# A two-layer hybrid trunk step on one core: bank pools of the FFN's products, the place of the residual sums and of LN1's last sums, small copies on ScalarE, an RMS root by ln and exp

## The chip, the cores and the metric

The kernel runs on one core of a Trainium2 chip. A core has five engines with a queue each: TensorE (PE, with its weight loads PEld), VectorE (DVE), ScalarE (ACT), GpSimd (POOL) and SyncE (SP). Each engine works its queue off in order; what an instruction needs from another engine it waits for on semaphores. The metric is the device time of one execution in microseconds.

## The reference, cut to what matters

One inference step of a decoder trunk of two layers, in fp32, on 1024 tokens of a new sequence and 8 x 4 sample tokens that continue from given states:

```python
for l in range(DEPTH):
    p = x @ w_in[l]
    p_rw, p_gl, p_rt = _split(p, (RWKV_COLS, GLA_COLS, RET_COLS))
    y_a, sh, s_a = _rwkv7_mix(p_rw, ...)      # 6 heads of 64
    y_b, s_b = _gla_mix(p_gl, ...)            # 5 heads, then _rms_heads, gate
    y_c, s_c = _ret_mix(p_rt, ...)            # 5 heads, then _rms_heads, gate
    mix = jnp.concatenate([y_a, y_b, y_c], axis=-1) @ w_out[l]
    x = _layer_norm(ALPHA * x + mix, ln1_g[l], ln1_b[l])
    f, cv = _conv_ffn(x, ...)
    x = _layer_norm(ALPHA * x + f, ln2_g[l], ln2_b[l])

def _rms_heads(o):
    return o * lax.rsqrt(jnp.mean(jnp.square(o), -1, keepdims=True) + RMS_EPS)

def _conv_ffn(x, conv0, w_up, conv_w, conv_b, w_down):
    u = x @ w_up                                             # 1024 -> 2 x 2816
    buf = jnp.concatenate([conv0.astype(u.dtype), u], axis=1)
    c = conv_b + sum(conv_w[j] * buf[:, j:j + t_] for j in range(CONV_W))   # 3 taps in time
    a, b = jnp.split(c, 2, axis=-1)
    return (jax.nn.gelu(a) * b) @ w_down, buf[:, -(CONV_W - 1):]
```

## The kernel before

**Tiles.** The 1056 tokens lie in three blocks of 384, 384 and 288 columns (the last holds 32 sample tokens and 256 prompt tokens); channels lie on partitions. An fp32 product is three matmuls (`mm3`, L130): each operand is a high part, cast on ACT, and a low part, the difference, taken mostly on POOL (`split`, L187). So a weight tile `wir` or `wU0r` becomes `...wh` (ACT) and `...wl` (POOL).

**Stages of a layer.** First the RWKV stage (chains of small products, `gps`, `tps`, `zy`), then the GLA and RetNet stage with the output projection (`ytp` turns the heads' outputs, `po` projects) and LayerNorm 1, then the FFN and LayerNorm 2. The input products of the GLA and RetNet columns (`gt`) are filler for PE in the first two stages.

**Who sets the order.** PE's order is written out at build time: generators (streams) yield either a delay from the table `AFTER` or an event, a clock `TE.t` adds up the matmuls' nominal time, and a stream goes on when its delay is over on that clock; meanwhile filler is issued. PE's instructions are chained in that order (`Tensor.order`). The queues of the other engines are ordered by the framework's scheduler, from its own simulation.

**LayerNorm 1.** Per block, `ln.add` sums a tile and its square on DVE and POOL (L931, L932), `ln.stats` has PE sum over the partitions (`lnm`, `lnv`), and `ln.apply` makes the normed block: DVE subtracts the mean (L956), takes the variance (L946), ACT makes the root by ln and exp (L947, L948, each with a table load here), DVE multiplies (L957), ACT scales (L958), and ACT and POOL split the result into `x1h` and `x1l`.

**RMS root.** `finish` takes an output of GLA or RetNet (`gop`, `rop`): ACT copies it and squares it, DVE sums per head (L976), and `rsqrt` (L228 to L234) makes the root on DVE in twelve operations on 128 x 5 values: a bit trick and three Newton steps. Then L980 and L981 multiply. There are 36 calls of `finish` in the program and 18 other calls of `rsqrt`, in the RWKV stage.

**FFN.** The 22 pairs of up tiles go two by two. Pairs 0 and 1 (`up_blocks`, products `pu`) are plain: per block, two tiles of 48 matmuls together. Then `residual` (L1442) puts `x1h + x1l` together in fp32 on POOL, sixteen 128 x 384 additions, and `sums` makes from these the operands of a scheme of seven products for four (blocks 0 and 1 times two weight halves). From pair 2 on, `up` runs the seven products `pa`, `pg`, `pb`, `pc`, `pf`, `pd`, `pe` and the sample block's `p0`, `p1`. The first product's tile `u` is added to the second, `pg`, by DVE at L1524; on `u` the three taps run (L1402 on ACT, L1398 on DVE), then gelu (L1431) and the gate (L1432), then the split into `hh` and `hl`. Behind `pg` of every second pair stand the `downs` of the two pairs before: 24 products `pd` of two pairs each, added to `acc` by DVE (L1594; the first group L1596). A down of block 0 or 1 is six matmuls, and the first four of a half are block 0's, the next four block 1's.

**Banks.** In the FFN PSUM has two pools: `pd` with five banks (all seven products and the downs) and `pg` with three (`pu` of blocks 0 and 1, `p0`, `p1`). A tile of a pool takes the banks in turn and waits until the bank's last reader is done.

**Halos.** The first two columns of a `u` are the last two of the tile before it in time (POOL copy L1394), or zero (POOL memset L1391), or come from the convolution's given state (`cvt`, POOL copy L1415).

**FFN weights.** They go through six buffers for `wh` and six for `wl`. Pair 0 has four pieces (`wU0`), so two of pair 1's (`wU1`) can be split at once and the others when PE gives up the first pieces.

Of the kernel before, what the change touches and what calls it, by code (L numbers as in the profile page):

```python
# [159 lines left out]
def step_kernel(ctx: ExitStack, tc: tile.TileContext, xT, wA, wB, wO, wU, wD, pp, pb, lora, bg, bgk, shT, cvT, srw, sgl, srt,  # L160
# [136 lines left out]
    for l in range(depth):  # L297
# [1090 lines left out]
        def halo(u, n, prev):  # L1388

            if n == 0:  # L1390
                G.memset(u[:, 0:2], 0.0)  # L1391
            else:
                o = 48 if n == 2 else 0
                G.tensor_copy(u[:, o:o + 2], prev[:, 384:386])  # L1394

        def taps(t, c, uu, cv, w):
            for tap in (1, 0):
                V.scalar_tensor_tensor(cv, uu[..., tap:tap + w], pc(PP_CV + 4 * t + tap), cv, ALU.mult, ALU.add)  # L1398
# [6 lines left out]
        def conv_prompt(t, i, u, src):  # L1405

            c = conv_start(t, i, src, 384)
            taps(t, c, u[:, 0:386], c, 384)
            return c

        def conv_samples(t, i, ps):
# [3 lines left out]
            G.tensor_copy(s[:, :, 0:2], cvt[:, t, 2:18].rearrange("p (b t) -> p b t", b=8))  # L1415
# [413 lines left out]
```

## Time and profile before

| | |
|---|---|
| median of 3 runs | 3508.7 us (3494.66 to 3511.85) |
| profiled execution, own time | 3504.8 us |
| its span | 3503.0 us |
| mean granted clock of TensorE | 0.936 |
| PE busy, 0 to 600 us | 554.97 us |
| PE busy, 600 to 916 us (GLA, RetNet, output, layer 0) | 276.27 of 316 us |
| PE busy, 916 to 1016 us (FFN entry, layer 0) | 81.28 of 100 us |
| PE busy, 1016 to 1700 us (FFN, layer 0) | 652.07 of 684 us |
| PE busy, 2650 to 2750 us (FFN entry, layer 1) | 79.18 of 100 us |
| PE busy, 2750 to 3450 us (FFN, layer 1) | 666.26 of 700 us |

A row of waits names the engine, the tile and line that waited, what it waited for, the total in us, how often, and the longest. In a timeline a bracket holds the idle time ahead of an instruction and what ended it.

### The profile page before, as it was taken

What the parts mean: (1) busy time and instruction counts of PE and PEld (TensorE: products, weight loads), DVE (VectorE), ACT (ScalarE), POOL (GpSimd) and SP (SyncE); (2) the same over time, 40 slices, a digit from 0 to 9 for tenths busy, and PEclk for the clock granted to TensorE, in tenths of its full rate; (3) what the DMA queues carried; (4) which work ended last, traced back from release to release, by engine and by line L of the source; (5) the groups of instructions that cost most, each with busy time, mean ns of one, the idle gap of its engine ahead of it and who ended that gap; (6) DMA issues with size and microseconds to landing.
All of it is one profiled execution on the core that took longest, in us unless ns stands there. A gap on an engine that the chain in (4) does not pass through costs nothing.

```text
span 3503.0 us, 59691 instructions
## 1 busy us (share of the span) xinstructions
PE 3184.6 (91%) x21630; PEld 2937.8 (84%) x21630; DVE 2445.3 (70%) x5493; ACT 1492.9 (43%) x3286; POOL 1680.2 (48%) x1876
## 2 busy tenths in 40 slices
PE   9889999988799999999888999999887999999995
PEld 8778888777799899989787888877777989999995
DVE  3587664677687767677946776647777786777778
ACT  6554332334543334333575533323345433433335
POOL 5442222133665555554765422221437655655566
PEclk9789999998999999999898899999898999999998
DMA  7343223343311111111264422243432111111111
GB/s 247 116 122 92 64 61 125 116 122 99 84 40 47 42 46 49 46 40 46 80 192 143 118 79 65 69 127 119 129 98 70 43 43 45 47 46 42 46 52 66
DMA packets 245570, 291.17 MB, mean 83 GB/s; under 512 B 76620, under 2 KB 158316, under 8 KB 245276
## 3 DMA queue, kind: packets, MB, share of 16 engines
q1 hardware_dynamic: 225004, 274.08, 25.7%
q10 hardware_dynamic: 20272, 13.29, 1.5%
q8 instruction: 170, 2.79, 0.3%
q14 instruction: 124, 1.02, 0.1%
HBM read 228.85 MB, written 58.43 MB: 82 GB/s over the span
## 4 chain that ended last, share of the span: by engine, by line
PE 52%; DVE 22%; POOL 7%; DMA 7%; issue 5%; ACT 4%; SPq 1%; ACTq 0%; DVEq 0%; POOLq 0%
PE pd L130 11%; PE gt L130 9%; PE pa L130 6%; PE p L130 4%; DVE c L1398 3%; DVE tm L622 2%; DVE U L624 2%; PE pb L130 2%; PE po L130 2%; PE gps L130 2%; DVE c L1432 2%; PE zy L130 1%; PE pf L130 1%; PE pc L130 1%; PE gop L130 1%
## 5 line engine op out<-in xcount | busy, mean ns | idle before, releaser
L1398 DVE SCALAR_TENSOR_TENSOR c<-u,ppt,c 128x32 f32<-128x32 f32 (+2 forms) x704 | 489.4, 731 | 145.2 <-ACT u L1416 64.1
L187 POOL TENSOR_TENSOR wil<-wir,wih 128x512 fp32r<-128x512 f32 (+1 forms) x264 | 368.1, 1402 | 352.9 <-ACT wih L187 342.2
L130 PE MATMUL gt<-wih,xh 128*128 128x320 f32 (+1 forms) x1008 | 341.3, 340 | 0.0
L130 PE MATMUL gt<-wil,xh 128*128 128x320 f32 (+1 forms) x1008 | 317.1, 316 | 6.6 <-POOL wil L187 6.6
L1594 DVE TENSOR_TENSOR acc<-acc,pd 128x384 f32<-128x384 f32 (+1 forms) x464 | 230.8, 516 | 98.8 <-PE pd L130 98.7
L130 PE MATMUL gt<-wih,xl 128*128 128x320 f32 x896 | 282.3, 315 | 0.0
L187 ACT CAST wih<-wir 128x512 fp32r<-128x512 f32 (+1 forms) x296 | 185.6, 637 | 166.6 <-PE po L130 69.6
L130 PE MATMUL pa<-xh,wih 128*128 128x384 f32 (+1 forms) x576 | 217.9, 378 | 19.3 <-DVE mx L380 8.8
L622 DVE TENSOR_TENSOR tm<-U,N 96x60 f32<-96x60 f32 (+24 forms) x558 | 176.4, 316 | 65.4 <-DMA N<-gd 46.4
L130 PEld LDWEIGHTS gt<-wih,xh 128*128 128x128 f32 (+1 forms) x1008 | 187.9, 186 | 37.0 <-issue 21.2
L130 PE MATMUL pa<-xl,wih 128*128 128x384 f32 (+1 forms) x576 | 203.0, 352 | 3.9 <-POOL xl L187 3.6
L130 PE MATMUL pa<-xh,wil 128*128 128x384 f32 (+1 forms) x576 | 202.4, 351 | 4.2 <-POOL wil L187 3.5
L130 PEld LDWEIGHTS gt<-wil,xh 128*128 128x128 f32 (+1 forms) x1008 | 189.4, 188 | 10.7 <-POOL wil L187 9.5
L624 DVE TENSOR_TENSOR U<-U,tm 96x60 f32<-96x60 f32 (+24 forms) x558 | 171.3, 307 | 14.4 <-DMA tokd<-ev 0.4
L130 PEld LDWEIGHTS gt<-wih,xl 128*128 128x128 f32 x896 | 173.9, 194 | 0.0
L1402 ACT ACTIVATE c<-u,ppt 128x384 f32<-128x384 f32 x160 | 113.2, 709 | 108.0 <-DVE u L1524 38.0
L187 POOL TENSOR_TENSOR hl<-c,hh 128x384 fp32r<-128x384 f32 x132 | 143.2, 1090 | 22.8 <-ACT hh L187 22.8
L130 PEld LDWEIGHTS pa<-xh,wih 128*128 128x128 f32 x576 | 121.2, 210 | 33.4 <-DVE mx L380 10.3
L130 PE MATMUL po<-yh,wih 128*128 128x384 f32 (+1 forms) x384 | 137.3, 358 | 13.0 <-DVE ac L1317 9.3
L130 PE MATMUL po<-yh,wil 128*128 128x384 f32 (+1 forms) x384 | 130.4, 339 | 3.8 <-DVE wil L187 3.8
L130 PE MATMUL po<-yl,wih 128*128 128x384 f32 (+1 forms) x384 | 130.1, 339 | 0.0
L130 PEld LDWEIGHTS pa<-xl,wih 128*128 128x128 f32 x576 | 121.8, 211 | 9.0 <-POOL xl L187 5.8
(955 smaller groups left out, 10425.3 us busy)
## 6 DMA issues: line engine op xcount, KB each, us to landing
wir<-in_wA_dram SPq DMA_DIRECT2D x144, 256.0 KB
wir<-in_wO_dram SPq DMA_DIRECT2D x96, 256.0 KB
wir<-in_wB_dram SPq DMA_DIRECT2D x56, 320.0 KB
tokd<-ev SPq DMA_DIRECT2D x112, 160.0 KB
x<-rkvd SPq DMA_DIRECT2D x16, 576.0 KB
tk<-tokd SPq DMA_DIRECT2D x16, 480.0 KB
rkvd<-mx SPq DMA_DIRECT2D x36, 192.0 KB
tk<-tokd SPq DMA_DIRECT2D x16, 400.0 KB
```

Source lines behind the costliest of these rows:

```text
L130: self.order(self.engine.matmul(out, lhsT, rhs, start=start, stop=stop), cols, 4 if rhs.dtype == F32 else 1)
L187: return A.copy(dst_h, src), (le or G).tensor_tensor(dst_l, src, dst_h.bitcast(F32), ALU.subtract)
L622: V.tensor_tensor(tm, U[:, 0:nr, i:i + 1].to_broadcast([4 * ns, nr, 31 - i]), N[:, i:i + 1, i + 1:32].to_broadcast([4 * ns, nr, 31 - i]), ...
L624: V.tensor_tensor(U[:, 0:nr, i + 1:32], U[:, 0:nr, i + 1:32], tm, ALU.add)
L1398: V.scalar_tensor_tensor(cv, uu[..., tap:tap + w], pc(PP_CV + 4 * t + tap), cv, ALU.mult, ALU.add)
L1402: A.activation(c, src, AF.Identity, scale=pc(PP_CV + 4 * t + 2), bias=pc(PP_CV + 4 * t + 3))
L1432: V.tensor_tensor(cs[1], cs[0], cs[1], ALU.mult)
L1594: V.tensor_tensor(a, a, ps, ALU.add)
```

## The change

It has these parts:

1. In `up` the second product `pg` takes its bank from the pool of three, with `p0` and `p1`; in `up_blocks` the products of blocks 0 and 1 take theirs from the pool of five, and those of block 2 from the pool of three.
2. `residual` is issued at the start of the second pair, after that pair's weights, not after the first pair's block 1.
3. The zero halo is left out: the two taps that reach before the sequence run on 383 and 382 columns. The other halos and the copy from the convolution's state go from POOL to ACT.
4. `finish` has ACT load a table set (`natural_log_exp_and_others`) behind the square, then take ln and exp of the sums. `rsqrt` stays for the RWKV stage.
5. LN1's sums over partitions of block 2 (`lnm`, `lnv`) are held back and put on PE behind the first pair's block 0, with no delay ahead of them.
6. In the planner's table, `operands` gets 5.5 more for blocks 0 and 1, and `x11` goes from 1.28 to 3.0.
7. LN2's sums take their banks from the pool of three in all blocks.

```diff
-AFTER = {... "operands": 8.0, ... "x11": 1.28, ...}
+AFTER = {... "operands": 8.0, "early": 5.5, ... "x11": 3.0, ...}
...
     def order(self, ins, cols, passes):
+        if self.held is not None:
+            self.held.append((ins, cols, passes))
+            return
...
+    def hold(self, do):
+
+        self.held = []
+        do()
+        held, self.held = self.held, None
+        return lambda: [self.order(*h) for h in held]
...
-            yield AFTER["operands"]
+            yield AFTER["operands"] + (AFTER["early"] if s.b < 2 else 0)
...
-            A.activation(sq, dst, AF.Square)
+            first = A.activation(sq, dst, AF.Square)
...
             V.tensor_reduce(sm, hv(sq), mybir.AxisListType.X, ALU.add)
-            sm = rsqrt(gp_, sm, 1.0 / 64, 1e-6)
+
+            ins = TE.after(A.preload_act_table_set("natural_log_exp_and_others"), first)
+            TE.after(A.activation(sm, sm, AF.Ln, scale=1.0 / 64, bias=eps(1, rows)), ins)
+            A.activation(sm, sm, AF.Exp, scale=-0.5)
...
-            yield AFTER["ln"]
-            ln.stats()
+            yield AFTER["ln"] if n < 2 else 0
+            if n < 2:
+                ln.stats()
+            else:
+                stats3.append(TE.hold(ln.stats))
...
         def halo(u, n, prev):
 
-            if n == 0:
-                G.memset(u[:, 0:2], 0.0)
-            else:
+            if n:
                 o = 48 if n == 2 else 0
-                G.tensor_copy(u[:, o:o + 2], prev[:, 384:386])
+                A.copy(u[:, o:o + 2], prev[:, 384:386])
 
-        def taps(t, c, uu, cv, w):
+        def taps(t, c, uu, cv, w, first=False):
             for tap in (1, 0):
-                V.scalar_tensor_tensor(cv, uu[..., tap:tap + w], pc(PP_CV + 4 * t + tap), cv, ALU.mult, ALU.add)
+                o = 2 - tap if first else 0
+                V.scalar_tensor_tensor(cv[..., o:], uu[..., tap + o:tap + w], pc(PP_CV + 4 * t + tap), cv[..., o:], ALU.mult, ALU.add)
...
-            G.tensor_copy(s[:, :, 0:2], cvt[:, t, 2:18].rearrange("p (b t) -> p b t", b=8))
+            A.copy(s[:, :, 0:2], cvt[:, t, 2:18].rearrange("p (b t) -> p b t", b=8))
...
         def up_blocks(j):
...
+            if j:
+                residual()
             for n in range(3):
...
-                    ps = bank(2, f"pu{t}")[:, :NB[n][1]] if n == 2 else pg.tile([P, 512], F32, tag="g", name=f"pu{t}")[:, :384]
+                    ps = bank(n, f"pu{t}")
...
-                if n == 1:
-                    qs = sums() if j else residual()
+                if n == 0 and j == 0:
+                    stats3[0]()
+                if n == 1 and j:
+                    qs = sums()
...
-            p2 = bank(0, "pg")
+            p2 = pg.tile([P, 512], F32, tag="g", name="pg")[:, :384]
             product(p2, w, b21)
             u11 = new_u()
-            halo(u11, 0, None)
...
-                lns[n].ps = lambda name: pg.tile([P, 512], F32, tag="g", name=name)
...
-            lns.append(LayerNorm(n, acc[n], (t[:, 0], t[:, 1]), lambda name: pd.tile([P, 512], F32, tag="d", name=name), (fp, "u", 6)))
+            lns.append(LayerNorm(n, acc[n], (t[:, 0], t[:, 1]), lambda name: pg.tile([P, 512], F32, tag="g", name=name), (fp, "u", 6)))
```

What the change does to the queues is not all to be seen in the code. Three places follow. The first is PE in layer 0, the fourth and the fifth down behind `pg` of pair 4 (weights of pairs 2 and 3; the brackets name the engines that a matmul waits for). Before:

```order
L130 MATMUL pd<-hh,wD2wh 128x384 [waits Activation_49]
L130 MATMUL pd<-hl,wD2wh 128x384
L130 MATMUL pd<-hh,wD2wl 128x384
L130 MATMUL pd<-hh,wD3wh 128x384
L130 MATMUL pd<-hl,wD3wh 128x384
L130 MATMUL pd<-hh,wD3wl 128x384
L130 MATMUL pd<-hh,wD2wh 128x384 [waits DVE_49]
L130 MATMUL pd<-hl,wD2wh 128x384
L130 MATMUL pd<-hh,wD2wl 128x384
L130 MATMUL pd<-hh,wD3wh 128x384 [waits Activation_49]
L130 MATMUL pd<-hl,wD3wh 128x384 [waits Pool_49]
L130 MATMUL pd<-hh,wD3wl 128x384
```

The fourth down takes the bank of `pa`, which ACT frees, the fifth that of `pg`, which DVE frees. The same two downs in the changed kernel:

```order
L140 MATMUL pd<-hh,wD2wh 128x384 [waits DVE_49]
L140 MATMUL pd<-hl,wD2wh 128x384
L140 MATMUL pd<-hh,wD2wl 128x384
L140 MATMUL pd<-hh,wD3wh 128x384
L140 MATMUL pd<-hl,wD3wh 128x384
L140 MATMUL pd<-hh,wD3wl 128x384
L140 MATMUL pd<-hh,wD2wh 128x384 [waits Activation_49]
L140 MATMUL pd<-hl,wD2wh 128x384
L140 MATMUL pd<-hh,wD2wl 128x384
L140 MATMUL pd<-hh,wD3wh 128x384 [waits Activation_49]
L140 MATMUL pd<-hl,wD3wh 128x384 [waits Pool_49]
L140 MATMUL pd<-hh,wD3wl 128x384
```

The bank of `pg` is out of the round and that of `pa` comes one down later; the fifth down's waits for the second pair's `hh` (ACT) and `hl` (POOL) stay. The second place is POOL at the FFN entry of layer 0, from the first pair's weights on (`x1l` of 128x288 is block 2's). Before:

```order
L187 TENSOR_TENSOR wU0wl<-wU0r,wU0wh 128x512 x4
L187 TENSOR_TENSOR wU1wl<-wU1r,wU1wh 128x512 x2
L187 TENSOR_TENSOR x1l_10295<-ac,x1h_10294 128x288 x8
L1359 COPY gb_10386<-ppt 128x16
L1391 MEMSET u 128x2 x2
L1442 TENSOR_TENSOR acc_10362<-x1h_9256,x1l_9257 128x384
...
L1442 TENSOR_TENSOR acc_10369<-x1h_9256,x1l_9257 128x384
L187 TENSOR_TENSOR hl<-c,hh 128x384
L1415 COPY u<-cvt 128x8x2
L1394 COPY u<-u 128x2
...
L187 TENSOR_TENSOR wU1wl<-wU1r,wU1wh 128x512 x2
```

All sixteen additions of `residual` stand ahead of the second pair's third and fourth weight. The same in the changed kernel:

```order
L197 TENSOR_TENSOR wU0wl<-wU0r,wU0wh 128x512 x4
L197 TENSOR_TENSOR wU1wl<-wU1r,wU1wh 128x512 x2
L197 TENSOR_TENSOR x1l_10079<-ac,x1h_10078 128x288 x8
L197 TENSOR_TENSOR wU1wl<-wU1r,wU1wh 128x512
L1376 COPY gb_10170<-ppt 128x16
L1458 TENSOR_TENSOR acc_10146<-x1h_9238,x1l_9239 128x384
...
L1458 TENSOR_TENSOR acc_10161<-x1h_9700,x1l_9701 128x384
L197 TENSOR_TENSOR wU1wl<-wU1r,wU1wh 128x512
L1458 TENSOR_TENSOR acc_10153<-x1h_9238,x1l_9239 128x384
```

The third weight now stands ahead of the additions, the fourth behind fifteen of them. The third place is ACT at the first `finish` of layer 0 (`yg`, GLA's output of one tile; `ev` at L875 is a gate of the input products, by tanh). Before, the square L974 is ACT's last part of it:

```order
L1034 COPY qT<-gtp 32x128
L972 COPY yg<-gop 128x320
L974 ACTIVATE rsq<-yg 128x320
L868 COPY ev<-gt 128x320
L1067 ACTIVATE upe<-gup,eb 128x64
L1067 ACTIVATE upe<-gup,eb 32x64
```

And in the changed kernel:

```order
L1047 COPY qT<-gtp 32x128
L982 COPY yg<-gop 128x320
L984 ACTIVATE rsq<-yg 128x320
L988 ACT_TABLE_LOAD
L989 ACTIVATE rsm<-rsm,cf 128x5
L875 ACT_TABLE_LOAD
L875 ACTIVATE ev<-gt 128x320
L990 ACTIVATE rsm<-rsm 128x5
L1080 ACTIVATE upe<-gup,eb 128x64
```

A table load and the ln follow the square, and here a gate's table load and its tanh come between ln and exp. Over the whole program ACT's rows hold 65 table loads before and 124 now; the twelve of LN1 are gone, 49 new ones lie at the lines of the root (L988 to L990), 16 at the gates (L875), and 6 in the RWKV stage.

More of the change, by code (lines that the diff above doesn't have):

```diff
@@ L34 @@
 GW = 320
-AFTER = {"key": 5.93, "sh": 3.5, "rkv": 2.0, "block": 6.0, "blockin": 2.5, "x": 3.0, "operands": 8.0, "gram": 0.9, "tv": 0.9, "tb": 0.9, "solve": 24.0, "ud": 4.5, "joined": 4.0, "mask": 1.5, "gd": 4.5, "x11": 1.28, "x21": 1.4, "x22": 0.6, "z": 1.4, "s": 1.58, "am": 2.0, "sx": 1.0, "sout": 3.0, "y": 7.3, "gate": 1.4, "state": 2.5, "done": 7.0, "turn": 2.5, "tokin": 3.36, "ev": 2.25, "gexp": 2.6, "gqt": 1.6, "rrot": 5.5, "rqt": 2.0, "at": 2.5, "qm": 0.8, "vx": 0.9, "gstate": 1.2, "tk": 4.5, "gateout": 4.0, "yin": 2.2, "yout": 4.5, "gnext": 1.2, "rout": 8, "rnext": 0.8, "yt": 0.5, "yready": 1.79, "ln": 3.0, "lnk": 1.5, "lns": 3.0, "ln1": 3.0, "ln2": 9.0}
+AFTER = {"key": 5.93, "sh": 3.5, "rkv": 2.0, "block": 6.0, "blockin": 2.5, "x": 3.0, "operands": 8.0, "early": 5.5, "gram": 0.9, "tv": 0.9, "tb": 0.9, "solve": 24.0, "ud": 4.5, "joined": 4.0, "mask": 1.5, "gd": 4.5, "x11": 3.0, "x21": 1.4, "x22": 0.6, "z": 1.4, "s": 1.58, "am": 2.0, "sx": 1.0, "sout": 3.0, "y": 7.3, "gate": 1.4, "state": 2.5, "done": 7.0, "turn": 2.5, "tokin": 3.36, "ev": 2.25, "gexp": 2.6, "gqt": 1.6, "rrot": 5.5, "rqt": 2.0, "at": 2.5, "qm": 0.8, "vx": 0.9, "gstate": 1.2, "tk": 4.5, "gateout": 4.0, "yin": 2.2, "yout": 4.5, "gnext": 1.2, "rout": 8, "rnext": 0.8, "yt": 0.5, "yready": 1.79, "ln": 3.0, "lnk": 1.5, "lns": 3.0, "ln1": 3.0, "ln2": 9.0}
 FB, BB = 2, 3
@@ L106, in __init__ @@
     def __init__(self, tc, engine):
-        self.tc, self.engine, self.t, self.last, self.posts = tc, engine, 0.0, None, []
+        self.tc, self.engine, self.t, self.last, self.posts, self.held = tc, engine, 0.0, None, [], None
         Event.clock = self.clock
@@ L1330, in out_projs @@
                 yield from out_proj(n)
+        stats3 = []
         ln1, ln1_at = [None] * 2, [Event() for _ in range(2)]
@@ L1403, in conv_start, with conv_prompt @@
             return c
-        def conv_prompt(t, i, u, src):
+        def conv_prompt(t, i, u, src, first=False):
             c = conv_start(t, i, src, 384)
-            taps(t, c, u[:, 0:386], c, 384)
+            taps(t, c, u[:, 0:386], c, 384, first)
             return c
@@ L1488, in up_blocks @@
                         A.copy(u[:, 2:386], ps)
-                        c = conv_prompt(t, i, u, ps)
+                        c = conv_prompt(t, i, u, ps, n == 0)
                     else:
@@ L1518, in up @@
                 c20, u20 = conv_samples(t0, 0, p0)
-            p2 = bank(0, "pg")
+            p2 = pg.tile([P, 512], F32, tag="g", name="pg")[:, :384]
             product(p2, w, b21)
             u11 = new_u()
-            halo(u11, 0, None)
             v11, v22 = u11[:, 2:386], u22[:, 2:386]
             V.tensor_tensor(v11, v22, p2, ALU.add)
-            c11 = conv_prompt(t0, 0, u11, v11)
+            c11 = conv_prompt(t0, 0, u11, v11, True)
             between()
@@ L1549, in up @@
             u21 = new_u()
-            halo(u21, 0, None)
             v21 = u21[:, 2:386]
@@ L1554, in up @@
             halo(u22, 1, u21)
-            hs = [up_gate((c11, conv_prompt(t1, 1, u21, v21)), 0)]
+            hs = [up_gate((c11, conv_prompt(t1, 1, u21, v21, True)), 0)]
             if not late:
```

## The prediction

> **What bounds the kernel now.** I read the page's busy line first, then TensorE's waits, then the places that these name. The busy line and the waits (columns: total us, times, longest us):
>
> ```profile
> PE 3184.6 (91%) x21630; PEld 2937.8 (84%) x21630; DVE 2445.3 (70%) x5493; ACT 1492.9 (43%) x3286; POOL 1680.2 (48%) x1876
> ```
>
> ```profile
> PE pd L130 <- DVE u L1524: 52.1, 20, 2.9
> PE ytp L133 <- DVE ac L1317: 17.2, 6, 5.9
> PE tps L130 <- ACT x L648: 15.6, 6, 4.9
> PE ytp L133 <- DVE yt L981: 14.5, 8, 3.7
> PE gps L130 <- DVE bk L525: 13.2, 4, 6.0
> PE pu L130 <- POOL wU1wl L187: 11.5, 2, 6.3
> ...
> PE lnm L130 <- DVE s L931: 9.7, 4, 3.0
> PE po L130 <- DVE ac L1317: 9.3, 4, 3.2
> ...
> PE pu L130 <- ACT c L1402: 7.4, 2, 4.1
> ```
>
> PE is busy for 91% of the span and its matmul count stays, so only PE's idle time, 3503.0 - 3184.6 = 318 us, can be won. It is scattered: the steady FFN's wait for `u` L1524 (52.1), the FFN entry (`wU1wl`, `c` L1402 and part of `s` L931), the RWKV stage (`tps`, `gps`), and the output side of GLA and RetNet (`ytp`, `po`). The change aims at each of them, so each is priced where it lies. All sums go against the profiled execution's own time, 3504.8 us (span 3503.0 and 1.8 around it), 0.1% below the median of 3508.7.
>
> **The steady FFN: second product in another pool.** One cycle as the timeline shows it (start, length, engine): DVE, POOL and PE around the stall at 1142.
>
> ```profile
> 1136.63 4.03 DVE L1398 SCALAR_TENSOR_TENSOR c<-u,ppt,c 128x384 f32<-128x384 f32 x6 [1.20 <-ACT c L1402]
> 1140.77 2.91 DVE L1432 TENSOR_TENSOR c<-c 128x384 f32<-128x384 f32 x2
> ...
> 1144.37 0.54 DVE L1524 TENSOR_TENSOR u<-u,pg 128x384 f32<-128x384 f32 x1
> ...
> 1145.88 0.54 DVE L1594 TENSOR_TENSOR acc<-acc,pd 128x384 f32<-128x384 f32 x1
> ```
>
> ```profile
> 1144.29 2.33 POOL L187 TENSOR_TENSOR hl<-c,hh 128x384 fp32r<-128x384 f32 x2
> ```
>
> ```profile
> 1144.97 0.44 PE L130 MATMUL pd<-hh,wD4wh 128*128 128x384 f32 x1 [2.72 <-DVE u L1524]
> 1145.25 0.33 PE L130 MATMUL pd<-hl,wD4wh 128*128 128x384 f32 x1
> ...
> 1145.94 0.34 PE L130 MATMUL pd<-hh,wD5wl 128*128 128x384 f32 x1
> 1146.48 0.44 PE L130 MATMUL pd<-hh,wD4wh 128*128 128x384 f32 x1 [0.20 <-DVE acc L1594]
> ```
>
> Four downs run (six matmuls each), the fifth stands 2.72 us for the bank of `pg`, which L1524 frees at 1144.91. With `pg` in the other pool the fifth down takes the bank of `pa`, long free, and this wait is gone. What is late next? The fifth down is the first that reads the second row of hidden tiles: its fifth matmul needs `hl`, whose split starts on POOL at 1144.29. That row holds two splits in 2.33 us, so the first ends near 1145.3. Four matmuls (4 x 0.173 us, by the four from 1145.25 to 1145.94) get ahead of the stall, and the fifth starts at 1145.3 instead of 1145.94 - 0.173 = 1145.77. The sixth down needs the bank of the first, which `acc` at 1145.88 frees at 1146.42: it starts at 1146.48 in either kernel. These times are set by DVE, which has worked without a break since 1136.63, and its order there is the same row for row. So the stall changes its name (to POOL `hl` and DVE `acc`) and keeps its end. Gain between 0.3 us a cycle, 6 us in 20, and nothing; I take 0, as DVE's row is the nearer one.
>
> **Halos on ScalarE.** These leave POOL; in their place ACT gets small copies, priced like its smallest copy here:
>
> ```profile
> L1394 POOL COPY u<-u 128x2 f32<-128x2 f32 x176 | 54.3, 323 | 15.2 <-DVE u L1524 11.7 <-ACT u L1488 2.9 <-DVE u L1553 0.6
> L1415 POOL COPY u<-cvt 128x16 f32<-128x16 f32 x88 | 31.3, 357 | 1.1 <-DVE x1l L1452 1.1
> ```
>
> ```profile
> L1416 ACT COPY u<-p 128x32 f32<-128x32 f32 x76 | 13.1, 173 | 0.0
> ```
>
> POOL loses 85.6 us, ACT gains 264 x 0.173 = 46 us, both in queues with idle time. The copy from another `u` waits for DVE's add (the 11.7 above), and now ACT's queue stands for it, with `hh` casts and weight casts behind. Within that bound (11.7 us lost) and a relief of DVE, whose operations beside POOL's are long, of 1 us a cycle (20 us won), I take 0.
>
> **The FFN entry.** Before, PE stops for block 2's sums, then for a bank, then for a weight half. The rows of PE and POOL:
>
> ```profile
> 919.77 1.33 PE L130 MATMUL lnm<-s,cf 128*128 128x288 f32 x2 [3.02 <-DVE s L931]
> ...
> 941.68 0.44 PE L130 MATMUL pu<-x1h,wU0wh 128*128 128x384 f32 x1 [3.32 <-ACT c L1402]
> ...
> 964.87 0.69 PE L130 MATMUL pu<-x1h,wU1wl 128*128 128x384 f32 x1 [6.34 <-POOL wU1wl L187]
> ```
>
> ```profile
> 938.07 4.76 POOL L187 TENSOR_TENSOR x1l<-ac,x1h 128x288 fp32r<-128x288 f32 x6 [0.46 <-ACT x1h L187]
> ...
> 942.98 14.38 POOL L1442 TENSOR_TENSOR acc<-x1h,x1l 128x384 f32<-128x384 f32 x13
> ...
> 963.56 2.50 POOL L187 TENSOR_TENSOR wU1wl<-wU1r,wU1wh 128x512 fp32r<-128x512 f32 x2
> ```
>
> And DVE's row behind `lnm`, and a window of PE behind the third stall (length, busy time and count of the five engines, granted clock):
>
> ```profile
> 921.57 8.47 DVE L956 TENSOR_TENSOR ac<-ac,s 128x288 f32<-128x288 f32 x8 [1.31 <-ACT s L944]
> 929.96 0.45 DVE L946 TENSOR_TENSOR s<-lnv,s 128x288 f32<-128x288 f32 x1
> ```
>
> ```profile
> 964.90:969.30 4.40, 4.40 (x14) 4.40 (x15) 4.40 (x3) 1.00 (x2) 4.40 (x9) 0.50 0.38 119
> ```
>
> A stall thus costs its length and some 2.2 us more, since PE runs 4.4 us at half clock behind it. The Trainium skill, "TensorE: Matmul & The Clock Gate" (What's actually happening), gives half speed after an idle window of about 3.4 us; the 6.34 us stall agrees.
>
> Taken as written, the change removes all three. Read by the new order, not so. The first pair's weights are cast right behind the last sums, at 919.8; PE starts near 921 (my estimate: a split of 1.25 us behind them), does a block's 48 matmuls (8.3 us at 0.173, plus 2.2 of slow clock), and the held sums follow at 931.5 instead of 919.77. From `lnm` to the last `x1l` it took 942.83 - 919.77 = 23 us; without POOL's weight splits beside it L956 falls from 8.47 to 8 x 0.45 = 3.6 us, and two table loads of LN1 (1.28 us each, row below) go, so 23 - 4.9 - 2.6 = 15.5: `x1` of block 2 is complete at 947. PE, done with block 1 at 940, now waits some 4 us for it. The third weight half then comes before the residual sums, but the fourth stands behind fifteen of them in POOL's queue: 947 + 1.3 + 15 x 14.38/13 + 1.3 = 966, and PE, which needs it near 957, stops for 9 us. Before, PE stood at 964.87 with two halves to go of this block, now at 966 with one of them done: 2 us ahead at best. Per layer I take 1 us, 2 in all; bounds are -8 (the fourth half 4 us later) and +30 for both layers (11.5 + 7.4 + 6 for two waits of 3.0 on `s`, and 5 of slow clock).
>
> **RMS root by ln and exp.** The durations of DVE's root (162 rows are three for each of 54 roots, 36 of them here), and of what comes:
>
> ```profile
> L233 DVE SCALAR_TENSOR_TENSOR nw<-nw,nw 128x5 f32<-128x5 f32 (+3 forms) x162 | 38.4, 237 | 3.1
> L232 DVE TENSOR_TENSOR nw<-nw 128x5 f32<-128x5 f32 (+3 forms) x162 | 36.4, 224 | 2.9
> L234 DVE SCALAR_TENSOR_TENSOR nw<-nw,nw 128x5 f32<-128x5 f32 (+3 forms) x162 | 34.3, 212 | 3.4 <-DVE U L624 0.2
> L230 DVE TENSOR_SCALAR nw<-nw 128x5 int32<-128x5 int32 (+3 forms) x54 | 20.7, 384 | 0.9
> L229 DVE TENSOR_SCALAR nw<-nw 128x5 int32<-128x5 int32 (+3 forms) x54 | 20.2, 373 | 0.4
> L947 ACT ACT_TABLE_LOAD x12 | 15.4, 1283 | 0.2
> 600.00:916.00 316.00, 276.27 (x2074) 233.04 (x2073) 229.56 (x548) 128.22 (x328) 107.51 (x88) 0.90 0.37 112
> ```
>
> DVE loses (38.4 + 36.4 + 34.3 + 20.7 + 20.2) / 54 = 2.78 us a root, 100 us in 36. ACT gets 72 activations near 0.17 us and, by the new order, 59 more table loads on balance: 59 x 1.283 = 76 us, in a stage where it works 128.2 of 316 us. The Trainium skill, "ScalarE: Activation LUTs" (What ACT_TABLE_LOAD costs), puts a switch at about 2.66 us with its drain; by that the loads would be 157 us. On the path of one root: the load (1.28 us, part of it beside the reduction), then Ln, Exp and hand-overs, by my estimate 1.5 us against 2.78; where a tanh gate's load falls between Ln and Exp, as in the rows of the change, about 3.2. DVE waits for that in its queue with the GLA state update `sg` behind it, so only part of its 100 us comes free. Of the waits on this side (17.2 + 14.5 + 9.3 = 41 us) I take an eighth, 5 us; the bounds are 25 won and 15 lost.
>
> **The planner's waits.** `early` gives two blocks of each layer 5.5 us more filler before `gps`, `x11` 1.72 us more before each `tps`. Where PE stood that long, filler takes the idle time: at most 13.2 + 6 x 1.72 = 23.5 us. The filler is not new, it is missing later, where the output side waits anyway, hence 0 at the other end. I take 14, nearer the top, as two of the four `gps` stalls (longest 6.0) are long enough to bring the slow clock too.
>
> The late sums and the pool of LN2's sums move no wait that ends last at the end of a layer: 0.
>
> **Sum:** -14 - 5 - 2 - 0 = -21; 3504.8 - 21 = 3483.8, and I say 3484.
>
> **The rivals.**
> *The steady stall is won.* If the reordered queues let DVE and `hl` come earlier, the 52.1 go: 3484 - 52 = 3432. For it: the wait's name is a bank. Against: `hl` and `acc` end 0.4 and 1.5 us later. Chance 0.14.
> *Nothing is left.* The filler is missed as much as it helped, `x1` and the fourth half take back the entry: 3504. For it: the new order of POOL. Chance 0.24.
> *Slower, by table loads.* ScalarE's queue holds the loads ahead of evictions that PE waits for. Each load on the path costs 1.283 us; 17 of the 59 eat the 21 us, 31 make it 0.5% slower, all give 3484 + 76 = 3560, 50 of them 3548. By the 2.66 us of the Trainium skill, "ScalarE: Activation LUTs" (What ACT_TABLE_LOAD costs), all 59 would give 3484 + 157 = 3641. For it: the loads lie on the chain to `ytp`. Against: ACT is idle for over half of this stage. Chance 0.14.
> *The forecast*, 3484, own range 3455 to 3508: 0.48.
>
> **How the numbers follow.** About 0.5% (17 us) is what a measurement of this kernel can tell from no change. Faster: 0.36 of the forecast's 0.48, all 0.14, 0.03 of "nothing": 0.53. Slower: the 0.14 and 0.01 of "nothing" and 0.01 of the forecast: 0.16. Same: 0.31. The range leaves out the better half of the first rival and most of the last: 3435 to 3522.
>
> **What would show it.** Right: `pd <- u L1524` gone, and `pd <- hl` and `pd <- acc` with some 50 us in its place; `pu <- wU1wl` still about 9 us a layer; a new wait `pu <- x1h` or `x1l`; `gps <- bk` small; POOL's L1394 gone. Wrong: the twenty FFN cycles shorter by 2 us each or more, the entry by 10, or PE waiting for ACT in the GLA stage.

## The result, and the profile after

| | before | after |
|---|---|---|
| median of 6 runs each | 3505.3 us | 3474.1 us |
| lowest and highest | 3494.7, 3517.3 | 3468.7, 3488.6 |
| ratio after to before, 95% interval | | 0.991 [0.989, 0.994] |
| profiled execution's span | 3503.0 us | 3474.6 us |

The change makes the kernel 0.9% faster, 28 us by the spans. The forecast was 3484 us in a range of 3435 to 3522. The sum came near, but its terms did not all: two were missed by much and in opposite directions.

The busy line of the page after:

```profile
PE 3164.5 (91%) x21630; PEld 2910.7 (84%) x21630; DVE 2350.8 (68%) x5061; ACT 1606.0 (46%) x3681; POOL 1594.4 (46%) x1524
```

DVE and POOL have lost 95 and 86 us of work and ACT has gained 113. PE's own busy time fell too, by 20 us with the same matmuls: less of it ran at half clock (mean granted clock 0.942, before 0.936). PE's idle time fell by 8 us only, from 318 to 310. PE's waits after, with the same columns as before:

```profile
PE pd L140 <- POOL hl L197: 38.9, 20, 2.1
PE pd L140 <- DVE acc L1612: 25.3, 35, 4.7
PE pu L140 <- POOL wU1wl L197: 22.1, 2, 11.0
PE ups L140 <- ACT x L663: 17.5, 7, 5.7
PE pg L140 <- ACT c L1418: 15.9, 2, 8.1
...
PE gp L140 <- ACT gm L668: 11.8, 5, 7.1
...
PE po L140 <- DVE ac L1330: 7.6, 4, 2.9
PE pu L140 <- ACT wU0wh L197: 7.3, 2, 3.7
...
PE lnm L140 <- DVE s L941: 3.5, 2, 1.8
...
PE ytp L143 <- DVE ac L1330: 3.3, 1, 3.3
```

Row by row against before: the 52.1 us for `u` are gone, `hl` is up from 3.7 to 38.9 and `acc` from 10.0 to 25.3; together 64.2 after 65.8. `wU1wl` has nearly doubled. `tps` (15.6) and `gps` on `bk` (13.2) are gone; `ups` and `gp` have come. Of the 31.7 us of `ytp` on `ac` and `yt`, 3.3 are left in this list. New are `pg` on `c` and `pu` on `wU0wh`.

Where the 28 us lie is read from the starts of products. The view of the tile `pu` in the first 1000 us gives, for its first weight, the number of matmuls, the shortest, median and longest in ns, and the first and last start. First before, then after:

```profile
L130 PE MATMUL pu<-x1h,wU0wh x48: 294/336/687, 922.1 to 953.5; 128*128 128x384 f32 x32, 128*128 128x288 f32 x16
```

```profile
L140 PE MATMUL pu<-x1h,wU0wh x48: 289/336/689, 895.9 to 925.9; 128*128 128x384 f32 x32, 128*128 128x288 f32 x16
```

So layer 0 reaches its FFN 26.2 us earlier. From the starts of the first `po`, the first and the last `pu` and the first `pa` of the FFN in each layer I cut the span in stretches, here and for the experiments (us; "entry" is first `pu` to first `pa`, "FFN" first `pa` to last `pu`, "front" what lies ahead of the first `pu`, in layer 1 from the last `pu` of layer 0 on; "output" is the part of a front from the first `po` on):

| | ratio to before [95%] | front 0 (output) | entry 0 | FFN 0 | front 1 (output) | entry 1 | FFN 1 |
|---|---|---|---|---|---|---|---|
| before | 1 | 922.1 (194.0) | 63.6 | 712.1 | 960.0 (180.5) | 62.8 | 711.2 |
| after | 0.991 [0.989, 0.994] | 895.9 (163.8) | 67.4 | 712.0 | 950.5 (164.3) | 67.9 | 709.9 |
| root_old | 0.997 [0.996, 0.999] | 900.3 (176.7) | 66.8 | 711.9 | 979.7 (190.4) | 68.9 | 712.4 |
| plan_old | 0.995 [0.994, 0.997] | 921.3 (178.2) | 66.9 | 712.6 | 947.0 (165.4) | 67.4 | 712.9 |
| root_plan_old | 1.002 [1.000, 1.004] | 926.9 (193.0) | 66.2 | 711.8 | 965.3 (180.6) | 66.8 | 712.8 |
| w4_first | 0.991 [0.989, 0.992] | 896.2 (166.7) | 54.1 | 726.8 | 948.2 (165.7) | 53.2 | 726.6 |
| pg_first | 0.990 [0.988, 0.991] | 893.1 (169.1) | 67.3 | 709.2 | 950.1 (165.5) | 67.6 | 709.3 |
| mend | 0.991 [0.989, 0.993] | 896.1 (166.8) | 53.6 | 730.6 | 941.9 (164.4) | 54.0 | 727.4 |
| sums_early | 0.987 [0.985, 0.989] | 895.8 (165.0) | 62.2 | 708.0 | 949.6 (166.8) | 62.4 | 710.0 |
| halo_pool | 0.992 [0.990, 0.994] | 891.5 (163.6) | 65.0 | 717.1 | 955.3 (164.7) | 65.0 | 715.4 |
| pg_back | 0.993 [0.990, 0.995] | 891.8 (164.2) | 67.4 | 712.1 | 950.7 (164.7) | 67.7 | 711.6 |
| sums_ln2 | 0.991 [0.988, 0.993] | 898.3 (170.6) | 61.8 | 711.1 | 949.4 (165.3) | 62.5 | 711.5 |
| best_first | 0.988 [0.985, 0.991] | 900.3 (170.8) | 61.8 | 712.0 | 940.3 (162.4) | 61.5 | 712.1 |
| best_back | 0.990 [0.987, 0.993] | 909.1 (168.1) | 62.0 | 712.7 | 953.0 (167.4) | 61.7 | 713.2 |

Both fronts together win 35.7 us, the entries lose 8.9, the FFN wins 1.4. The FFN column starts at the first `pa`, so the wait for the bank of `pg` (8.1 us in each layer after the change) lies in it.

Each row of the table is one execution, and these differ. Ten of the kernels (all but before, *root_old*, *plan_old* and *root_plan_old*) have the same order of PE's matmuls up to the first `po`, and still reach it between 724.0 and 741.0 us. Their outputs in layer 0 take 163.6 to 170.8 us and their fronts 0 come at 891.5 to 909.1. The kernel before reaches the first `po` at 728.1 and the changed one at 732.1, so the whole win of front 0 shows in the output stage. The profiled executions of *root_old*, *plan_old*, *root_plan_old* and *best_back* were 7 to 16 us above the median of their kernel, and their stretches are too long by that much in sum.

### The profile page after: what moved, and what is told of

It reads as the page before. It is cut to its first block, busy times and chain, and to the rows that moved or that the text cites. A ratio compares the mean times of both kernels' runs of the same rounds, so it can differ in the third digit from the quotient of the medians.

```text
span 3474.6 us, 59233 instructions
## 1 busy us (share of the span) xinstructions
PE 3164.5 (91%) x21630; PEld 2910.7 (84%) x21630; DVE 2350.8 (68%) x5061; ACT 1606.0 (46%) x3681; POOL 1594.4 (46%) x1524
## 5 line engine op out<-in xcount | busy, mean ns | idle before, releaser
L1414 DVE SCALAR_TENSOR_TENSOR c<-u,ppt,c 128x32 f32<-128x32 f32 (+3 forms) x704 | 495.8, 739 | 139.0 <-ACT c L1418 134.7
L140 PE MATMUL pa<-xh,wih 128*128 128x384 f32 (+1 forms) x576 | 212.3, 368 | 23.6 <-DVE mx L390 11.8
L632 DVE TENSOR_TENSOR tm<-U,N 96x60 f32<-96x60 f32 (+24 forms) x558 | 164.2, 294 | 86.3 <-DMA N<-gd 71.8
L140 PEld LDWEIGHTS pa<-xh,wil 128*128 128x128 f32 x576 | 118.6, 206 | 10.6 <-POOL wil L197 9.9
```

The costliest lines, as they stand in the source:

```text
L140: self.order(self.engine.matmul(out, lhsT, rhs, start=start, stop=stop), cols, 4 if rhs.dtype == F32 else 1)
L632: V.tensor_tensor(tm, U[:, 0:nr, i:i + 1].to_broadcast([4 * ns, nr, 31 - i]), N[:, i:i + 1, i + 1:32].to_broadcast([4 * ns, nr, 31 - i]), ...
L1414: V.scalar_tensor_tensor(cv[..., o:], uu[..., tap + o:tap + w], pc(PP_CV + 4 * t + tap), cv[..., o:], ALU.mult, ALU.add)
```

## The experiments

All are edits of the changed kernel, timed in five rounds against the kernel before.

**The root and the delays.** *root_old* takes the root back to DVE:

```diff
-            ins = TE.after(A.preload_act_table_set("natural_log_exp_and_others"), first)
-            TE.after(A.activation(sm, sm, AF.Ln, scale=1.0 / 64, bias=eps(1, rows)), ins)
-            A.activation(sm, sm, AF.Exp, scale=-0.5)
+            sm = rsqrt(gp_, sm, 1.0 / 64, 1e-6)
```

> The changed kernel (3474 us, ratio 0.991 to before) with one part undone: the RMS root is again twelve DVE operations, without table loads. Two theories of where the 28 us came from. Root theory: they came from the GLA and RetNet stage, where DVE lost 100 us of work; then this kernel gives most of them back, the first pu matmul of layer 0 comes at 915 to 922 us instead of 895.9, and the time is 3500 to 3515. Planner theory, the one of the prediction: 14 us are the two delays and 5 the root; then the first pu comes near 899 and the time is 3475 to 3482.

Measured: 0.9972, that is 0.6% or 20 us given back. By this ratio its time is 3495 us, between the two theories and nearer the root's. The first wait of its list that is not in the changed kernel's:

```profile
PE ytp L143 <- DVE yt L991: 30.6, 8, 7.2
```

With the delays kept and the root on DVE this wait is twice that of before (14.5), while `ytp` on `ac` is 4.5 in place of 17.2; the two together are 35.1 us, 31.7 before, and 3.3 in the changed kernel. The outputs take 13 and 26 us longer. The first `pu` came at 900.3, where the planner theory had it, but this execution reached its first `po` at 723.6, 8.5 us ahead of the changed kernel's, at the early end of the ten. So the root theory holds for the place, not quite for the size, and the prediction's 5 us do not hold.

One more thing comes back with this edit: ACT's twelve table loads of LN1, which the changed kernel does without (71 loads in all, in place of 124). Four of the twelve lie in the entries, which are within 1 us of the changed kernel's. The run does not tell the other eight from the root; the wait for `yt` is the root's own chain.

*plan_old* sets the two delays back:

```diff
-AFTER = {... "early": 5.5, ... "x11": 3.0, ...}
+AFTER = {... "early": 0.0, ... "x11": 1.28, ...}
```

> The changed kernel with the two delays of the planner's table back to the old values (early 0, x11 1.28). Planner theory: some 14 us are given back, 3485 to 3492, with waits gps on bk of 13 us and tps on x of 15 us back. Root theory: in the changed kernel the wait on x only moved from tps (15.6 us before) to ups (17.5 us) and gp (1.7 to 11.8 us), so the delays are worth nothing: 3470 to 3478.

Measured: 0.9953, 0.4% or 14 us given back, the planner theory's number (by the two intervals it can be 2 to 26). Its waits:

```profile
PE tps L140 <- ACT x L658: 17.2, 6, 4.9
PE gps L140 <- DVE bk L535: 12.3, 4, 6.0
```

They are back as expected. In its profile front 0 is 25 us longer and front 1 3.5 us shorter, which is within what executions differ. The first `po` comes at 743.1, 2 us behind the last of the ten; the output takes 14 us longer than the changed kernel's and 7 longer than the longest of the ten. What this theory did not say is that the part of the loss that shows beyond the spread lies in the output stage, behind all the delays. That stage in the changed kernel and in *plan_old* (length, then busy time and count of PE, PEld, DVE, ACT and POOL, then granted clock):

```profile
732.10:895.90 163.80, 142.18 (x936) 124.89 (x935) 119.39 (x181) 88.77 (x187) 82.77 (x65) 0.95 0.42 127
```

```profile
743.10:921.30 178.20, 154.06 (x923) 135.06 (x922) 122.11 (x189) 91.98 (x184) 84.39 (x69) 0.89 0.39 119
```

PE is busy 12 us longer there, with 13 matmuls fewer and at a clock of 0.89 in place of 0.95; its idle time is only 2.5 us longer.

*root_plan_old* undoes both.

> The changed kernel with both the root and the two planner delays undone; what is left are the pools, the residual, the halos and the late sums. Undone alone, the root cost 0.6% and the delays 0.4%. If these are separate, this kernel is at 1.001 of before (3508 to 3518) since the FFN entry has lost some 9 us of PE time and the rest little. If root and delays need each other (the delays take filler from the output side, which only pays where the root has made it fast), it is faster than the one with the root alone undone: 0.993 to 0.997.

Measured: 1.002. The two are separate within the intervals: 0.6 and 0.4% alone, 1.1% together. What is left of the change, pools, residual, halos and late sums, is no gain; with an interval of 1.000 to 1.004 it is a small loss, if anything.

**The FFN entry.** *w4_first* makes the additions wait for the fourth weight's split in POOL's queue (an order, no semaphore):

```diff
-            split(p[0], p[1], raw)
+            cut[:] = split(p[0], p[1], raw)[1:]
...
-                    G.tensor_tensor(acc[n][m], x1[n][0][:, m].bitcast(F32), x1[n][1][:, m].bitcast(F32), ALU.add)
+                    TE.after(G.tensor_tensor(acc[n][m], x1[n][0][:, m].bitcast(F32), x1[n][1][:, m].bitcast(F32), ALU.add), cut[0])
```

> The changed kernel with the sixteen residual additions of POOL made to stand behind the split of the second pair's fourth weight half, which they overtook. If that place in POOL's queue costs the two waits pu on wU1wl (11.0 us each, and some 2 us of slow clock behind each): the waits go, and the time is 3446 to 3455. If POOL's sum of work at the FFN entry decides, the additions and the operands behind them only come later and the waits move to pg, pa or pd: 3468 to 3476.

Measured: 0.9907 and 3478 us, no gain. Yet the waits for `wU1wl` are gone, and PE reaches `pa` 13 to 15 us earlier. There it stops:

```profile
978.35 0.69 PE L140 MATMUL pg<-x1h,a12wh 128*128 128x384 f32 x1 [21.46 <-ACT c L1418]
```

It starts `pg` at 978.35, later than the changed kernel at 976.80. All of the win is given back at the next wait.

*pg_first* gives `pg` of pair 2 alone a bank of the other pool:

```diff
-            p2 = pg.tile([P, 512], F32, tag="g", name="pg")[:, :384]
+            p2 = bank(0, "pg") if j == 2 else pg.tile([P, 512], F32, tag="g", name="pg")[:, :384]
```

> The changed kernel with the product pg of the first seven-product pair alone (pair 2) back in the pool of five banks; all other pg stay in the pool of three. If the new wait of 8 us a layer (pg on ACT c L1418) is the bank that the second pair's last sample product holds, it goes with this, and 12 to 20 us are won: 3454 to 3462. If the late ACT activation behind it holds PE in any case (by pd or hh), the wait moves on and the time is 3470 to 3476.

Measured: 0.9896, within the interval of the changed kernel. The 8 us are gone; in the FFN 2.8 and 0.6 us are left of them. The second theory holds.

*mend* is both edits.

> Both edits to the FFN entry at once: the residual additions behind the fourth weight half, and pg of pair 2 alone in the pool of five. The fourth half first took the two waits of 11 us away and gave them back as a wait of 21.4 us for pg's bank, 978 us into the run, so its time stayed. If that bank was all, both gains add: from the first pu to the first pa 53 us as with the one edit and no 21 us stall behind it, 22 to 28 us faster than the changed kernel, a ratio to before of 0.983 to 0.985. If the work of ACT, DVE and POOL on the operands at this place is the bound, the wait moves to pd (hh, hl or acc) and the ratio stays at 0.988 to 0.992.

Measured: 0.9909, no gain. With neither the weight nor the bank in the way PE waits for the hidden tiles and for `acc`, in pieces; some of its timeline rows:

```profile
965.69 0.69 PE L140 MATMUL pd<-hh,wD1wl 128*128 128x384 f32 x1 [2.37 <-POOL wD1wl L197]
...
975.31 0.69 PE L140 MATMUL pd<-hh,wD0wh 128*128 128x384 f32 x1 [2.43 <-DVE acc L1616]
989.37 0.61 PE L140 MATMUL pd<-hh,wD1wh 128*128 128x288 f32 x1 [6.58 <-ACT hh L197]
```

Entry and FFN together take 784.2 and 781.4 us against 779.4 and 777.8. So at the entry the work of ACT, DVE and POOL on the residual, the operands and the hidden tiles sets the pace, and a wait of PE that is taken away there comes back at the next product.

*sums_early* puts LN1's last sums back ahead of the first product:

```diff
-            yield AFTER["ln"] if n < 2 else 0
-            if n < 2:
-                ln.stats()
-            else:
-                stats3.append(TE.hold(ln.stats))
+            yield AFTER["ln"]
+            ln.stats()
...
-                if n == 0 and j == 0:
-                    stats3[0]()
```

> The changed kernel with LN1's sums of block 2 back ahead of the FFN's first product, with their delay. If holding them back is worth what the prediction took for it (the wait of 3.0 us on s a layer, paid back by the later x1): within 0.15% of the changed kernel, a ratio of 0.990 to 0.993. If the weight casts, which now come behind the sums' copy, make PE start later: a ratio of 0.993 to 0.996, with the first pu 3 us later in each layer.

Measured: 0.9869, faster than both theories had it, and the lowest ratio of all. The entries are 5.2 and 5.5 us shorter than the changed kernel's, the first `pu` comes at the same time. Its row, and the changed kernel's at this place:

```profile
893.85 0.97 PE L140 MATMUL lnm<-s,cf 128*128 128x288 f32 x2 [2.79 <-DVE s L941]
```

```profile
895.87 0.69 PE L140 MATMUL pu<-x1h,wU0wh 128*128 128x384 f32 x1 [3.71 <-ACT wU0wh L197]
```

The wait of 2.8 us for the sums is not saved by holding them: PE stands 3.7 us for the first weight's cast, which lies behind the squares of those sums on ACT. It is late by the same tile, and the sums' matmuls now come on top later.

**Halos and pools.** *halo_pool* gives the copies back to POOL; the memsets stay out:

```diff
-                A.copy(u[:, o:o + 2], prev[:, 384:386])
+                G.tensor_copy(u[:, o:o + 2], prev[:, 384:386])
...
-            A.copy(s[:, :, 0:2], cvt[:, t, 2:18].rearrange("p (b t) -> p b t", b=8))
+            G.tensor_copy(s[:, :, 0:2], cvt[:, t, 2:18].rearrange("p (b t) -> p b t", b=8))
```

> The changed kernel with the halo copies and the copies of the convolution's state back on POOL (the memsets stay out). Prediction: nothing, a ratio of 0.990 to 0.993, and the same 64 us of waits of pd. If the relief of POOL and DVE is worth 1 us a cycle: 20 us slower, 0.996 to 0.998.

Measured: 0.9917, as the prediction had it. But its FFN is 5.1 and 5.5 us longer in the profile, and its entries 2.4 and 2.9 us shorter. The longer FFN is not the steady one. In each layer the 5 us are at its start, where the first `pg` waits for its bank, 13.4 us in place of 8.1:

```profile
975.29 0.69 PE L140 MATMUL pg<-x1h,a12wh 128*128 128x384 f32 x1 [13.37 <-ACT c L1418]
```

The waits of `pd` on `hl` and `acc` are 59.6 us after 64.2. So the copies on ScalarE are worth some 5 us of net time in the profiles, at the entries of the two layers, less than the ratio can tell.

*pg_back* gives all `pg` banks of the pool of five:

```diff
-            p2 = pg.tile([P, 512], F32, tag="g", name="pg")[:, :384]
+            p2 = bank(0, "pg")
```

> The changed kernel with pg of all pairs back in the pool of five banks. Prediction: the pool is worth nothing in the steady FFN; then the wait is again pd on u with some 50 us, the time from the first pa to the last pu stays at 710 to 713 us a layer, and only the wait of 8 us for pg's bank at the entry goes: a ratio of 0.988 to 0.991. Rival: the halos on ScalarE won 5 us a layer there (halo_pool took 717 and 715 us against 712 and 710) and the pool lost as much; then this kernel takes 705 to 708 us a layer, and the ratio is 0.985 to 0.988. If the pool is worth something: 715 us or more, 0.992 to 0.995.

Measured: 0.9927 [0.990, 0.995], above the 0.988 to 0.991 of the prediction's theory and in the range of the one by which the pool is worth something; its interval reaches into both ranges and takes in the changed kernel's 0.991. The FFN takes 712.1 and 711.6 us, as the prediction's theory had it. Its waits:

```profile
PE pd L140 <- DVE u L1543: 50.3, 18, 2.9
...
PE pd L140 <- DVE acc L1612: 19.5, 26, 4.1
```

The old name is back with the old size, and the time is the same within the interval. Beside *pg_first*, which has this edit for pair 2 alone, the FFN is 2.9 and 2.3 us longer; in *best_back* beside *best_first*, below, it is 0.7 and 1.1. So the pool is worth at most some 3 us a layer and not the 26 of the wait, and the prediction's reading of the steady stall is shown to that extent.

**A faster version.** *sums_ln2* is *sums_early* with LN2's sums in the pools of before:

```diff
+                lns[n].ps = lambda name: pg.tile([P, 512], F32, tag="g", name=name)
                 lns[n].stats()
...
-            lns.append(LayerNorm(n, acc[n], (t[:, 0], t[:, 1]), lambda name: pg.tile([P, 512], F32, tag="g", name=name), (fp, "u", 6)))
+            lns.append(LayerNorm(n, acc[n], (t[:, 0], t[:, 1]), lambda name: pd.tile([P, 512], F32, tag="d", name=name), (fp, "u", 6)))
```

> The changed kernel with LN1's late sums undone (which alone gave a ratio of 0.987) and LN2's sums back in the pools of before. From the last pu of layer 0 to the first po of layer 1 the changed kernel takes 786 us and before 780. If LN2's banks are part of that: 780 to 783 us, and a ratio of 0.984 to 0.986. If not, as the prediction had it: 0.986 to 0.988.

Measured: 0.9906 [0.988, 0.993], slower than either theory had it, and 0.4% above *sums_early*, from which it differs in LN2's banks alone; the two intervals just overlap. From the last `pu` of layer 0 to the first `po` of layer 1 it takes 784 us, but the changed kernel and its variants that leave this stretch as it is have 777.5 to 790.6, and before had 780. What LN2's banks are worth stays open.

*best_first* joins *sums_ln2* and *pg_first*, with the planner's delays in layer 0 only:

```diff
-            yield AFTER["operands"] + (AFTER["early"] if s.b < 2 else 0)
+            yield AFTER["operands"] + (AFTER["early"] if s.b < 2 and l == 0 else 0)
...
-            yield AFTER["x11"]
+            yield (AFTER["x11"] if l == 0 else 1.28)
```

> Put together from the runs so far: late sums undone, LN2's banks as before, pg of pair 2 alone in the pool of five, and the planner's delays in layer 0 only (in layer 1 the changed kernel lost 3.5 us by them). If the gains add: 0.980 to 0.984. If each only moves the next wait: 0.986 to 0.988, as with the sums alone.

*best_back* is the same with the edit of *pg_back* in place of that of *pg_first*.

> The same with pg of all pairs in the pool of five. If the pool is worth nothing: as best_first within 0.1%. If it costs 5 us a layer: 0.3% faster than best_first; if it is worth as much, 0.3% slower.

Measured: 0.9876 [0.985, 0.991] and 0.9898 [0.987, 0.993]. Both are faster than the kernel before; *best_first* has the lowest median (3461 us), but its interval overlaps those of the changed kernel and of *sums_early*. In its profile the entries are 6 us shorter each than the changed kernel's. Its front 1 is 10 us shorter, but *mend*, which keeps the delays in both layers, has 8.6 us of that too, and *best_back*, without them in layer 1, is 2.5 us longer. The gains do not add up as hoped, and that the version is faster than the changed kernel is likely, not shown.

## Why the prediction was right, and where its terms were not

**Steady FFN: 0 forecast, 1.4 us measured; the mechanism as told.** One cycle of the changed kernel, POOL and PE:

```profile
1124.61 2.32 POOL L197 TENSOR_TENSOR hl<-c,hh 128x384 fp32r<-128x384 f32 x2
```

```profile
1125.68 0.44 PE L140 MATMUL pd<-hl,wD5wh 128*128 128x384 f32 x1 [2.11 <-POOL hl L197]
1126.79 0.44 PE L140 MATMUL pd<-hh,wD4wh 128*128 128x384 f32 x1 [0.50 <-DVE acc L1612]
```

Four matmuls get ahead, the fifth stands 2.11 us for `hl`, the next down 0.50 us for `acc`: the stall kept its end and changed its name. *pg_back* shows the counterpart. The 1.4 us are of stretches that hold the entry's new wait for the bank of `pg` too, worth 2.8 and 0.6 us by *pg_first*. In this the name of the longest wait (a bank) was the wrong thing to remove.

**The planner's delays: 14 forecast, 14 measured** (*plan_old*), though only in part by the mechanism given. The forecast put filler into PE's idle time, and went near the top because two of the `gps` stalls bring the slow clock. The idle time was not won: where PE had stood for `gps` and `tps` (13.2 and 15.6 us) it now stands for `ups` and `gp`, 17.5 and 11.8 us. The clock differs. In layer 0 before, two stalls for `gps` of 5.96 and 5.47 us, at 98.6 and 141.6 us, were followed by 17.8 and 15.8 us at a clock of 0.50. The clock in 100 to 200 us is the last but two of these columns; before, after, and with the delays undone (*plan_old*):

```profile
100.00:200.00 100.00, 88.08 (x535) 78.21 (x534) 65.29 (x172) 52.17 (x112) 45.17 (x50) 0.80 0.42 124
```

```profile
100.00:200.00 100.00, 88.29 (x595) 78.17 (x594) 70.58 (x185) 61.17 (x128) 56.22 (x62) 0.88 0.47 142
```

```profile
100.00:200.00 100.00, 88.53 (x532) 78.92 (x531) 64.33 (x168) 51.09 (x109) 46.11 (x50) 0.79 0.43 124
```

PE is busy for 88 us in all three, and does 595 matmuls (not all of one size) in place of 535 and 532, at a clock of 0.88 in place of 0.80 and 0.79. This is no chance of one execution: the eleven kernels with the delays have 0.83 to 0.91 here, the three without 0.79 to 0.80. So filler in the two stalls kept the clock up, though a stall of 5.5 us for `mx` has come at 139.7. But the first `po` does not come earlier for it beyond what executions differ. The loss that *plan_old* shows lies in layer 0's output stage and is mostly slower clock as well (0.89 for 0.95). Why the delays raise the clock that far behind them is not settled, so that the number fits is in part luck.

**The root: 5 forecast, 20 measured** (*root_old*). The term that was mis-sized is the root's price before: "2.78 us a root" is what its operations are busy (3.01 with L228, which the sum left out), and I set that against 1.5 to 3.2 us of path on ACT. But they stood in DVE's queue between other work. One root before, from the sum over heads (L976) to the first use (L980):

```profile
750.67 0.47 DVE L976 TENSOR_REDUCE rsm<-rsq 128x5 f32<-128x320 f32 x1
...
751.75 0.15 DVE L228 TENSOR_SCALAR nw<-rsm 128x5 f32<-128x5 f32 x1
751.93 0.55 DVE L1317 SCALAR_TENSOR_TENSOR ac<-xr,po 128x384 f32<-128x384 f32 x1
752.40 5.05 DVE L229 TENSOR_SCALAR nw<-nw 128x5 int32<-128x5 int32 x1
...
760.02 0.17 DVE L234 SCALAR_TENSOR_TENSOR nw<-nw,nw 128x5 f32<-128x5 f32 x1
760.10 0.55 DVE L1317 SCALAR_TENSOR_TENSOR ac<-xr,po 128x384 f32<-128x384 f32 x1
760.57 0.48 DVE L980 TENSOR_TENSOR yt<-yt,nw 128x320 f32<-128x320 f32 x1
```

And the same place after:

```profile
758.49 0.47 DVE L986 TENSOR_REDUCE rsm<-rsq 128x5 f32<-128x320 f32 x1
...
761.05 1.62 DVE L941 TENSOR_TENSOR s<-ac 128x384 f32<-128x384 f32 x1
762.59 1.57 DVE L993 TENSOR_TENSOR yt<-yt,rsm 128x320 f32<-128x320 f32 x1
```

Here 9.4 us pass before and 3.6 after; over all 36 roots taken in order, from the end of the sum to the start of the first use, the mean is 8.2 us before and 3.6 after (longest 30.2 and 8.4). This chain leads to `ytp`, and its waits were what *root_old* brought back; how much of the 20 us is LN1's table loads is not known. The table loads came as counted, 49 on the lines of the root:

```profile
L988 ACT ACT_TABLE_LOAD x36 | 46.2, 1283 | 0.6
...
L989 ACT ACT_TABLE_LOAD x7 | 9.0, 1283 | 0.1
L990 ACT ACT_TABLE_LOAD x6 | 7.7, 1283 | 0.1
```

They take their 1.28 us and no engine's long wait: the rival by table loads did not come. The Trainium skill, "ScalarE: Activation LUTs" (What ACT_TABLE_LOAD costs), adds a drain of some 1.38 us to each. The trace does not show one. In these rows the load starts 0.02 us behind the square's end, and the next activation starts 0.02 us behind the load's; so it is, within 0.02 us on either side, in 48 of the 49:

```profile
756.33 0.48 ACT L984 ACTIVATE rsq<-yt 128x320 f32<-128x320 f32 x1
...
756.83 1.28 ACT L988 ACT_TABLE_LOAD   x1
758.13 0.53 ACT L937 ACTIVATE s<-ac 128x384 f32<-128x384 f32 x1
```

**The FFN entry: 2 us won forecast, 9 lost measured,** one us beyond the lower bound. Three steps of it were right: the third weight came first and the fourth behind fifteen additions, and PE stopped for it, 11.0 us a layer where 9 were forecast. The wait for block 2's `x1`, forecast at some 4 us, was 0.9 us. POOL's rows:

```profile
922.70 1.60 POOL L197 TENSOR_TENSOR wU1wl<-wU1r,wU1wh 128x512 fp32r<-128x512 f32 x1
...
924.73 18.10 POOL L1458 TENSOR_TENSOR acc<-x1h,x1l 128x384 f32<-128x384 f32 x15
942.79 1.26 POOL L197 TENSOR_TENSOR wU1wl<-wU1r,wU1wh 128x512 fp32r<-128x512 f32 x1
```

Two steps were missing. The held sums make block 2's `x1` later and save nothing, as the cast of the first weight waits for the same tile (5 us a layer by *sums_early*). And `pg` of pair 2 now needs a bank of the small pool, which the last plain product holds until ACT reaches its `c`, behind the operands' casts: 8.1 us. That second wait costs little by itself, by *pg_first*, and *mend* shows why: behind it the other engines are late anyway. I had looked at each removed stall and not at what these engines have to do between the first `pu` and the first downs.

**The halos: 0 forecast,** and the time says no more; beside *halo_pool*, ScalarE's copies win some 5 us at the entries of the two layers in the profiles, and none in the steady FFN.

So the sum of the forecast, 21 us, met 28 measured because the root's 15 us too few and the entry's 11 too many nearly cancelled; that it came so near is in part luck. One premise was wrong as well: the prediction took it that only PE's idle time can be won, though it priced the slow clock behind some stalls. Of the 28 us by the spans 8 are idle time, and 20 are PE's busy time, which the higher clock made shorter.

## What to carry to other kernels

A wait's name says which semaphore came last, not what a removal would bring: look up what the same engine needs next, and when that is ready; here 52 us of waits for a bank were worth at most some 3 us a layer, and *w4_first*, *pg_first* and *mend* at the FFN entry only passed a wait on. Price a chain of small operations by the time from its first input to its last output in the queue where it stands, not by its busy time: twelve operations of 3.0 us took 8.2 us of queue. And where a stall is filled, count the matmuls behind it too: here the granted clock of a stretch of 100 us rose from 0.80 to 0.88 with the same busy time.

## What the runs showed of the hardware

A DVE operation on five values a partition, L229, took 5.05 us at 752.40 in the kernel before (its row is above), where its median is 0.16. POOL's rows at this time, and PE's wait at the end of this chain:

```profile
751.90 0.85 POOL L1125 TENSOR_TENSOR qk<-qk,tk 32x320 f32<-32x320 f32 x1 [0.43 <-DVE nw L228]
752.72 1.28 POOL L187 TENSOR_TENSOR wil<-wir,wih 128x512 fp32r<-128x512 f32 x1
753.97 1.00 POOL L932 TENSOR_TENSOR s<-s,sq 128x384 f32<-128x384 f32 x1
754.94 2.48 POOL L187 TENSOR_TENSOR wil<-wir,wih 128x512 fp32r<-128x512 f32 x2
```

```profile
760.71 0.47 PE L133 MATMUL ytp<-cs,yt 128*128 128x128 f32 x1 [4.96 <-DVE ac L1317]
```

POOL worked without a break from 751.90 to 757.42, and DVE's operation ended with it, at 757.45. The view of the line has the shortest, median and longest in ns:

```profile
L229 DVE TENSOR_SCALAR nw<-nw x54: 149/164/5048, 214.9 to 2597.6; 128x5 int32<-128x5 int32 x32, 128x6 int32<-128x6 int32 x16, 32x5 int32<-32x5 int32 x4, 32x6 int32<-32x6 int32 x2
```

The same shows in a full tile: at the FFN entry the eight subtractions of the mean took 8.47 us beside POOL's weight splits before, and 3.04 us after, with POOL idle:

```profile
908.66 3.04 DVE L966 TENSOR_TENSOR ac<-ac,s 128x288 f32<-128x288 f32 x8 [12.87 <-ACT s L954]
```

The other small operations of the root bear this out. The kernel before has 648 of them (twelve in each of 54 roots). Of the 588 that took less than 0.25 us, 22 ran beside any work of POOL. All 51 that took 0.6 us or more ran beside POOL for at least 96% of their length, and each ended 17 to 33 ns after the end of a POOL operation. Of the 51, 49 met one or two operations of POOL; the two longest, of 5.05 and 5.04 us, met five and ended with the fifth.

That DVE waits for POOL's access to the memory is what this looks like; no run took POOL's work away alone to show it.
